# Gated unit of a two-layer encoder: seven products of quarters in place of eight

## The chip, the cores and the metric

The kernel runs on one core of a Trainium2 chip. The metric is the device time of one execution in microseconds. TensorE (PE) does the matmuls and reads its weights through a separate load (PEld). VectorE (DVE), ScalarE (ACT) and GpSimd (POOL) do the elementwise work, and SyncE (SP) issues every transfer, in order.

## The reference, cut to what matters

The input x has 1024 tokens of 1024 channels in float32. Layer 0 runs a state-space branch (S5) and a retention branch side by side; layer 1 is a convolution module. The changed part is the gated unit at the end of the S5 branch:

```python
y = jax.nn.gelu(y)
y = y * jax.nn.sigmoid(y @ glu_w + glu_b)      # 1024 x 1024 weights
...
y_s5 = y_s5 * jax.nn.silu(g_s5)
y_ret = retention(q, k, v) * jax.nn.silu(g_ret)
return jnp.concatenate([y_s5, y_ret], axis=-1) @ w_out
```

## The kernel before, in words

Channels lie on the 128 partitions and tokens along the free axis, in two halves of 512. A block is 128 channels, so 1024 channels are eight blocks. Each float32 product is made of three matmuls: every operand is split into a rounded high part and the rest as a low part, and `mm3` (L161) issues high x high, high x low and low x high into one PSUM bank. `gemm` (L171) does so for the eight k-blocks: 24 matmuls of 128x512 for an output block of one token half.

Weights come through `wnext`, `wload` and `wload_pieces` (L109 to L160): one block of 512 KB at a time, loaded into `wf`, rounded to `wh` by ACT (L158), and its low part `wl` made by GpSimd, or by DVE for some names (L159). Each of the three has three buffers, and `wnext` issues loads two blocks ahead along the list that `plan` writes out.

The retention (`retention`, L864) runs four pairs of heads. `ret_proj` projects k and q, multiplies them out of PSUM into `kraw` and `qraw` (DVE, L913), and `turn` rotates them: four swap transfers into `swp`, products on GpSimd (L926, L928), an addition on DVE (L929). `ret_heads` then transposes k, evicts it as `kt` (L998), forms the states (`kv`, L1015), the scores (`sp`), masks them (`sc`, L1038), and makes the outputs `ro`, normalises them and stores them to `yr_d`. `y_pass` (L855) rides along, two blocks a pair: it loads the S5 output from `y_d`, applies gelu on ACT (L861) and stores it to `yn_d`.

The gated unit (L1141 to L1155) follows. Its operands, the blocks of `yn_d`, are loaded through the weight staging buffers and split into 16 + 16 tiles of `opA` (tag `A0` for the first token half, `A1` for the second) as soon as the last value projection lets those tiles go; low parts of the second half stand behind the last pair's `kt` and first mask. For each of eight output blocks and two halves, `gemm` fills one of three `mm` banks. Beside it SP loads `yg` (the SiLU gate, two buffers) and `yn` (three buffers), and GpSimd multiplies them (L1146). Then ACT takes tanh of the bank (L1150) into `sg`, DVE multiplies (L1151), ACT rounds the half of it to the high part (L1153) and DVE makes the low part (L1154). At the end the retention output is loaded from `yr_d` and split into the same `opA` tiles, and `w_out` (L1163) multiplies both by their halves of the output projection, an output block at a time.

The order of instructions on each engine is set by a planner that simulates the program: it takes ready work by program order, and `issue_after(x)` keeps what it encloses behind x.

## Time and profile before

| | us |
|---|---|
| median of 3 runs | 1202.06 (1201.37 to 1202.63) |
| the profiled execution | 1200.1 |
| its span, first to last instruction | 1198.3 |
| PE, DVE, ACT, POOL busy | 1188.7, 802.9, 477.8, 638.0 |
| first and last matmul of the gated unit start | 547.0, 646.0 |

The granted TensorE clock was 0.999 of full speed. Matmul records overlap one another, so a busy PE is not a measure of its rate; the starts of following matmuls are. In windows and timelines times are counted from the start of the span.

### The profile page before, as it was taken

The numbers are of one execution on the slowest core, as the hardware profiler recorded it, in microseconds if no ns is written. First come the engines' busy times: TensorE is split into PE (matmuls) and PEld (weight loads), VectorE is DVE, ScalarE is ACT, GpSimd is POOL, SyncE is SP. The second block draws the span as 40 slices with busy tenths as digits, with TensorE's granted clock in tenths as the row PEclk, the third lists the DMA queues.
The fourth block names the chain that finished last, engine by engine and source line by source line (L and its number), as shares of the span: only waits on it lengthen the run. The fifth ranks groups of instructions, "written<-read, shape, count | busy, mean of one in ns | idle before, by whom it ended". The sixth has DMA issues, their size and how long they took to land.

```text
span 1198.3 us, 17247 instructions
## 1 busy us (share of the span) xinstructions
PE 1188.7 (99%) x6424; PEld 996.2 (83%) x6424; DVE 802.9 (67%) x1388; ACT 477.8 (40%) x700; POOL 638.0 (53%) x442
## 2 busy tenths in 40 slices
PE   9999999999999999999999999999999999999997
PEld 7788888888888889998888888888888888888877
DVE  7975798777421557447655332599999799999533
ACT  6322232223223223144335322545535575434563
POOL 2059999987146254242441110678453567757643
PEclk9999999999999999999999999999999999999999
DMA  9344355564395175477547885765678654356774
GB/s 349 99 137 135 123 165 179 175 180 160 108 290 176 53 220 156 152 215 255 163 148 260 307 270 195 247 210 207 210 251 277 206 185 157 117 178 230 239 278 154
DMA packets 105220, 234.19 MB, mean 195 GB/s; under 512 B 9520, under 2 KB 40112, under 8 KB 104496
## 3 DMA queue, kind: packets, MB, share of 16 engines
q1 hardware_dynamic: 105136, 233.09, 59.2%
q8 instruction: 50, 0.82, 0.3%
q14 instruction: 34, 0.28, 0.1%
HBM read 166.80 MB, written 62.06 MB: 191 GB/s over the span
## 4 chain that ended last, share of the span: by engine, by line
PE 95%; DVE 2%; ACT 1%; DMA 1%; issue 1%; POOL 0%; SPq 0%; DVEq 0%; POOLq 0%; ACTq 0%
PE mm_g L167 8%; PE mm_g L168 7%; PE mm_g L169 7%; PE mm_wo L169 5%; PE mm_wo L167 5%; PE mm_wo L168 5%; PE mm_glu L167 2%; PE mm_b L168 2%; PE mm_b L169 2%; PE mm_glu L169 2%; PE mm_a L168 2%; PE mm_a L169 2%; PE mm_glu L168 2%; PE mm_b L167 2%; PE mm_a L167 2%; PE mm_oc L168 2%
## 5 line engine op out<-in xcount | busy, mean ns | idle before, releaser
L1274 DVE SCALAR_TENSOR_TENSOR cv<-u,convw,cv 128x512 f32<-128x512 f32 x398 | 273.3, 749 | 11.9 <-ACT cv L1260 9.6
L1254 POOL TENSOR_TENSOR tp<-tp,tp 128x512 f32<-128x512 f32 x64 | 82.9, 1296 | 44.1 <-ACT tp L1253 43.1
L167 PE MATMUL mm_g<-xh,wh_g 128*128 128x512 f32 x256 | 101.8, 398 | 0.0
L169 PE MATMUL mm_g<-xh,wl_g 128*128 128x512 f32 x256 | 100.1, 391 | 0.0
L168 PE MATMUL mm_g<-xl,wh_g 128*128 128x512 f32 x256 | 100.0, 391 | 0.0
L1253 ACT ACTIVATE tp<-u,convw 128x512 f32<-128x512 f32 x64 | 45.7, 720 | 35.3 <-POOL tp L1254 33.6
L396 POOL TENSOR_TENSOR s1q<-s1q,s1q 128x512 f32<-128x512 f32 x12 | 17.3, 1438 | 78.6 <-ACT s1q L391 78.6
L167 PEld LDWEIGHTS mm_g<-xh,wh_g 128*128 128x128 f32 x256 | 48.0, 188 | 11.7 <-issue 1.2
L169 PEld LDWEIGHTS mm_g<-xh,wl_g 128*128 128x128 f32 x256 | 48.0, 188 | 10.4
L168 PEld LDWEIGHTS mm_g<-xl,wh_g 128*128 128x128 f32 x256 | 48.1, 188 | 9.9 <-issue 0.4
L168 PE MATMUL mm_oc<-zl,wh_woc 128*128 128x512 f32 (+1 forms) x152 | 54.4, 360 | 0.5 <-POOL zl L1099 0.5
L169 PE MATMUL mm_oc<-zh,wl_woc 128*128 128x512 f32 (+1 forms) x152 | 53.9, 358 | 0.2 <-DMA wl_woc<-lo_woc 0.2
L167 PE MATMUL mm_oc<-zh,wh_woc 128*128 128x512 f32 (+1 forms) x152 | 54.1, 361 | 0.0
L1146 POOL TENSOR_TENSOR yg<-yg,yn 128x512 f32<-128x512 f32 x16 | 22.0, 1379 | 57.9 <-DMA yg<-gs_d 21.1
L352 DVE TENSOR_TENSOR gt<-mm_g,R 128x512 f32<-128x512 f32 x32 | 21.8, 682 | 43.6 <-PE mm_g L169 43.6
L167 PE MATMUL mm_g<-h1h,wh_cg 128*128 128x512 f32 x128 | 50.4, 394 | 0.0
L167 PE MATMUL mm_glu<-yh,wh_glu 128*128 128x512 f32 x128 | 50.3, 393 | 0.0
L167 PE MATMUL mm_wo<-yrh,wh_wor 128*128 128x512 f32 x128 | 50.2, 392 | 0.0
L167 PE MATMUL mm_b<-h1h,wh_cb 128*128 128x512 f32 x128 | 50.2, 392 | 0.0
L169 PE MATMUL mm_a<-h1h,wl_ca 128*128 128x512 f32 x128 | 50.2, 392 | 0.0
L169 PE MATMUL mm_wo<-yrh,wl_wor 128*128 128x512 f32 x128 | 49.9, 390 | 0.0
L168 PE MATMUL mm_b<-h1l,wh_cb 128*128 128x512 f32 x128 | 49.9, 390 | 0.0
(415 smaller groups left out, 3610.9 us busy)
## 6 DMA issues: line engine op xcount, KB each, us to landing
wf_g<-w_ab SPq DMA_DIRECT2D x16, 512.0 KB
wf_wos<-w_out SPq DMA_DIRECT2D x16, 512.0 KB
wf_wor<-w_out SPq DMA_DIRECT2D x16, 512.0 KB
wf_cb<-w_c SPq DMA_DIRECT2D x16, 512.0 KB
wf_ca<-w_c SPq DMA_DIRECT2D x16, 512.0 KB
wf_woc<-w_out_c SPq DMA_DIRECT2D x16, 512.0 KB
wf_v<-w_v SPq DMA_DIRECT2D x12, 512.0 KB
wf_cg<-w_c SPq DMA_DIRECT2D x11, 512.0 KB
```

What stands on the lines that cost most here:

```text
L167: nc.tensor.matmul(ps, wh[:, kb, :], xh, start=start, stop=False)
L168: nc.tensor.matmul(ps, wh[:, kb, :], xl, start=False, stop=False)
L169: self.last_mm = nc.tensor.matmul(ps, wl[:, kb, :], xh, start=False, stop=stop)
L352: nc.vector.tensor_tensor(gt[:, c], ps[:], self.R[:, c], op=ALU.mult)
L396: nc.gpsimd.tensor_tensor(a, a, sq[:], op=ALU.add)
L1146: gp.tensor_tensor(yg[:], yg[:], yn[:], op=ALU.mult)
L1253: nc.scalar.mul(sk[:], u[:, k:k + HALF], cw[:, nb, k:k + 1])
L1254: gp.tensor_tensor(s0[:], s0[:], sk[:], op=ALU.add)
L1274: v.scalar_tensor_tensor(dst[:], *tap, accs_[i][:], op0=ALU.mult, op1=ALU.add)
```

## The change

The 1024 x 1024 weights are cut into four quarters of 512 x 512, and y into four quarters: two halves of channels (b1., b2.) by two halves of tokens (b.1, b.2). The product is then formed by Winograd's variant of Strassen's scheme: seven products of quarters, with sums of quarters as operands, instead of eight. One product of quarters is four output blocks by four k-blocks, 48 `mm3` matmuls, for one token half's worth of 512 columns.

What is moved, added and removed:

- The weight list holds 14 blocks in place of 8: two (`m`) for each of seven products. A block of 512 KB now holds two output blocks (`a`) by four k-blocks, so it serves 24 matmuls in place of 48. Eight of the 14 are sums, read from a DRAM buffer `ws_d`; six are quarters as given.
- `glu_sums` makes the sums of the weights: for each of four groups two loads of 512 KB, four DVE operations of 128x512, two stores of 512 KB. Two groups come in the first pair and two in the third. They use the `swp` and `raw` buffers between rotations, and their DVE work stands behind the last raw eviction.
- `y_pass` handles blocks k and k + 4 together: k = 0 and 1 in the first pair, 2 in the third, 3 in the fourth, none in the second. After the gelu, DVE forms four sums of 128x512 and splits two results of 128x1024 into high and low parts, which are stored in `t_d` (four stores of 512 KB). The split of k = 1 stands behind the first pair's second mask.
- The retention's mask and k decay are loaded per pair.
- The gated unit runs the products in the order 1, 2 (both halves m), 6, 7, 4, then 5 and 3. Products 1 and 2 share their banks, as do 5 and 3; product 1 is copied out by ACT (`u2`) before product 2 is added. Products 6 and 7 are added to `u2` and `u3` by DVE, product 4 is subtracted from `u3` in a spare bank. `gated` works in the bank: tanh, DVE product and half are all written to PSUM or read from it, but for two blocks.
- The operands t1 to t4 come ready split from `t_d` (eight loads of 256 KB each); y11, y21 and y22 are loaded from `yn_d` and split as before.
- `w_out`'s first block takes its k-blocks in plain order.

```diff
-        seq += [(A["w_glu"][nb], f"glu{nb}") for nb in range(8)]
+        self.ws_d = self.dram.tile([2, 2, P, 2, KB, P], F32, name="ws_d")
+        quad = lambda i, j, m: A["w_glu"][i, m, :, j]
+        sums = lambda n, m: self.ws_d[n // 2, m, :, n % 2]
+        glu = [q for m in range(2) for q in (quad(0, 0, m), quad(0, 1, m))]
+        glu += [q(m) for q in (lambda m: sums(0, m), lambda m: sums(2, m), lambda m: quad(1, 1, m)) for m in range(2)]
+        glu += [sums(n, m) for m in range(2) for n in (3, 1)]
+        seq += [(q, f"glu{i}") for i, q in enumerate(glu)]
...
+    def mm3(self, ps, w, kb, x, start, stop, more=False):
...
-    def y_pass(self, rp, cb):
+    def y_pass(self, rp, k):
         nc = self.nc
-        yt = rp.tile([P, 8, P], F32, name=f"yp_{cb}", tag="yp", bufs=1)
-        nc.sync.dma_start(yt[:], self.y_d[cb].rearrange("i h g m -> (h g) i m"))
-        yn = rp.tile([P, P, 8], F32, name=f"yn_{cb}", tag="ynt", bufs=1)
-        nc.scalar.activation(yn[:], yt[:].rearrange("p i m -> p m i"), AF.Gelu_apprx_tanh)
-        nc.sync.dma_start(self.yn_d[cb * P:(cb + 1) * P], yn[:].rearrange("p m i -> p (m i)"))
+        yns = []
+        for i, cb in enumerate((k, k + 4)):
+            yt = rp.tile([P, 8, P], F32, name=f"yp_{cb}", tag="yp", bufs=1)
+            nc.sync.dma_start(yt[:], self.y_d[cb].rearrange("i h g m -> (h g) i m"))
+            yn = rp.tile([P, P, 8], F32, name=f"yn_{cb}", tag="ynt", bufs=2)
+            nc.scalar.activation(yn[:], yt[:].rearrange("p i m -> p m i"), AF.Gelu_apprx_tanh)
+            yn = yn[:].rearrange("p m i -> p (m i)")
+            nc.sync.dma_start(self.yn_d[cb * P:(cb + 1) * P], yn)
+            yns.append(yn)
+        (b11, b12), (b21, b22) = ((y[:, :HALF], y[:, HALF:]) for y in yns)
+        v = nc.vector
+        with self.tc.issue_after(self.last_raw.ins):
+            v.tensor_tensor(b22, b22, b12, op=ALU.subtract)
+            v.tensor_tensor(b12, b12, b11, op=ALU.subtract)
+            v.tensor_tensor(b11, b22, b11, op=ALU.add)
+            v.tensor_tensor(b21, b11, b21, op=ALU.subtract)
+        yield
+        for i in range(2):
+            hi = rp.tile([P, T], F32R, name=f"th{i}_{k}", tag="yp", bufs=1)
+            v.tensor_copy(hi[:], yns[i])
+            v.tensor_tensor(yns[i].bitcast(F32R), yns[i], hi[:].bitcast(F32), op=ALU.subtract)
+            nc.sync.dma_start(self.t_d[i, 0, k * P:(k + 1) * P], hi[:].bitcast(F32))
+            nc.sync.dma_start(self.t_d[i, 1, k * P:(k + 1) * P], yns[i])
+    def glu_sums(self, g, tag):
+        nc, v = self.nc, self.nc.vector
+        m, c = g // 2, slice(g % 2 * 4, g % 2 * 4 + 4)
+        q = [self.rq.tile([P, T], F32, name=f"gs{i}_{g}", tag=tag, bufs=2)[:].rearrange("p (j n) -> p j n", j=2)
+             for i in range(2)]
+        for i in range(2):
+            nc.sync.dma_start(q[i], self.A["w_glu"][i, m, :, :, c].rearrange("p j k n -> p j (k n)"))
+        (a11, a12), (a21, a22) = ((t[:, 0, :], t[:, 1, :]) for t in q)
+        with self.tc.issue_after(self.last_raw.ins):
+            v.tensor_tensor(a22, a21, a22, op=ALU.add)
+            v.tensor_tensor(a21, a11, a21, op=ALU.subtract)
+            v.tensor_tensor(a11, a22, a11, op=ALU.subtract)
+            v.tensor_tensor(a12, a12, a11, op=ALU.subtract)
+        with self.tc.issue_after(self.last_swap.ins):
+            for i in range(2):
+                nc.sync.dma_start(self.ws_d[i, m, :, :, c].rearrange("p j k n -> p j (k n)"), q[i])
     def retention(self, st):
         nc, A = self.nc, self.A
...
+            for g, tag in (((0, "swp"), (1, "raw")), (), ((2, "swp"), (3, "raw")), ())[pair]:
+                self.glu_sums(g, tag)
...
-                for cb in (2 * pair, 2 * pair + 1):
-                    self.y_pass(rq, cb)
+                parts = [self.y_pass(rq, k) for k in ((0, 1), (), (2,), (3,))[pair]]
+                for i, p in enumerate(parts):
+                    next(p)
+                    if i == 0:
+                        next(p, None)
+            if pair == 0:
+                with self.tc.issue_after(self.masked[1].ins):
+                    next(parts[1], None)
+        mask = rp.tile([P, 2, P], F32, name=f"retmask_{pair}", tag="retmask", bufs=2)
+        nc.sync.dma_start(mask[:], A["ret_mask"][:, 2 * pair:2 * pair + 2])
+        kdec = rp.tile([P, 2, 64], F32, name=f"kdec_{pair}", tag="kdec", bufs=2)
+        nc.sync.dma_start(kdec[:], A["ret_kdec"][:, 2 * pair:2 * pair + 2])
...
-        ys_in = load_split(self.yn_d, "y", False)
-        for nb, h in [(nb, h) for nb in range(6) for h in range(2)] + [(6, 0), (7, 0), (6, 1), (7, 1)]:
-            ps = self.bank(f"mm_glu{nb}_{h}", aux=False)
-            self.gemm(ps[:], ws[nb], ys_in[h])
-            sg = lp.tile([P, HALF], F32, name=f"sg{nb}_{h}", tag="u", bufs=5)
-            v.scalar_tensor_tensor(sg[:], sg[:], 1.0, yg[:], op0=ALU.add, op1=ALU.mult)
-            glu_end = v.scalar_tensor_tensor(b[:], sg[:], 0.5, a[:].bitcast(F32), op0=ALU.mult, op1=ALU.subtract)
-        yr = load_split(self.yr_d, "yr", True)
+        def load_split(parts, name, h, wide, behind=None):
+            res = []
+            for i, part in enumerate(parts):
+                if wide:
+                    if i % 2 == 0:
+                        f2 = self.wp.tile([P, 2, HALF], F32, name=f"{name}f{i}", tag="wf", bufs=3)
+                    f = f2[:, i % 2, :]
+                else:
+                    f = lp.tile([P, HALF], F32, name=f"{name}f{i}", tag="tp", bufs=3)[:]
+                nc.sync.dma_start(f, part)
+                a, b = (self.op_tile(self.opA, f"A{h}", f"{name}{q}{i}") for q in "hl")
+                self.split(f, a, b, v, behind)
+                res.append((a, b))
+        B = lambda j, h: [self.yn_d[rows(4 * j + k), hs(h)] for k in range(4)]
+        def load_sum(name, i, c, h):
+            res = []
+            for k in range(4):
+                ops = [self.op_tile(self.opA, f"A{h}", f"{name}{q}{k}") for q in "hl"]
+                for j, o in enumerate(ops):
+                    nc.sync.dma_start(o[:].bitcast(F32), self.t_d[i, j, rows(k), hs(c)])
+                res.append(ops)
+            return res
+        b11, b21 = load_split(B(0, 0), "y11", 0, True), load_split(B(1, 0), "y21", 0, True, self.masked[0])
+        u2 = [lp.tile([P, HALF], F32, name=f"gu2_{n}", tag=tag, bufs=1) for n, tag in enumerate(("cq", "cs", "pilot", "sq"))]
+        u3 = [opB.tile([P, HALF], F32, name=f"gu3_{n}", tag="B1") for n in range(4)]
+        nw = iter(range(14))
+        wn = lambda: self.wnext(f"glu{next(nw)}")
+        def product(ps, w, a, x, more=False):
+            for k in range(4):
+                self.mm3(ps[:], w, 4 * a + k, (x[k][0][:], x[k][1][:]), k == 0 and not more, k == 3, more)
+        def gated(nb, h, z):
+            src = z
+            if h == 0 and nb < 2:
+                z = lp.tile([P, HALF], F32, name=f"sg{nb}_{h}", tag="u", bufs=5)
+            nc.scalar.activation(z[:], src[:], AF.Tanh, scale=0.5, bias=hgb[:, nb:nb + 1])
+            v.scalar_tensor_tensor(z[:], z[:], 1.0, yg[:], op0=ALU.add, op1=ALU.mult)
+            nc.scalar.mul(a[:], z[:], 0.5)
+            return v.scalar_tensor_tensor(b[:], z[:], 0.5, a[:].bitcast(F32), op0=ALU.mult, op1=ALU.subtract)
+        def spare(name, n):
+            return ps_cv.tile([P, HALF], F32, name=name, tag=("cv", "cn")[n % 2])
+        for m in range(2):
+            pss = [self.bank(f"mm_glu1{2 * m + a}", aux=False) for a in range(2)]
+            for i, x in ((1, b11), (2, b21)):
+                w = wn()
+                if i == 1:
+                    t2, t3 = (load_sum("yt2", 0, 0, 1), None) if m == 0 else (t2, load_sum("yt3", 1, 1, 1))
+                for a in range(2):
+                    product(pss[a], w, a, x, i == 2)
+                    if i == 1:
+                        nc.scalar.copy(u2[2 * m + a][:], pss[a][:])
+                    else:
+                        gated(2 * m + a, 0, pss[a])
+        t4 = load_sum("yt4", 1, 0, 0)
+        for i, x in ((6, t2), (7, t3), (4, t4)):
+            for m in range(2):
+                w = wn()
+                for a in range(2):
+                    n = 2 * m + a
+                    ps = spare(f"mm_glu{i}{n}", n) if i == 4 else self.bank(f"mm_glu{i}{n}", aux=False)
+                    product(ps, w, a, x)
+                    if i == 4:
+                        v.tensor_tensor(ps[:], u3[n][:], ps[:], op=ALU.subtract)
+                        gated(4 + n, 0, ps)
+                    else:
+                        v.tensor_tensor((u2 if i == 6 else u3)[n][:], u2[n][:], ps[:], op=ALU.add)
+            if i == 6:
+                t1, b22 = load_sum("yt1", 0, 1, 0), load_split(B(1, 1), "y22", 1, False)
+        for m in range(2):
+            pss = [self.bank(f"mm_glu5{2 * m + a}", aux=False) for a in range(2)]
+            for i, x in ((5, t1), (3, b22)):
+                w = wn()
+                for a in range(2):
+                    n = 2 * m + a
+                    product(pss[a], w, a, x, i == 3)
+                    if i == 5:
+                        z = spare(f"mm_gluz{n}", n)
+                        v.tensor_tensor(z[:], u3[n][:], pss[a][:], op=ALU.add)
+                        gated(4 + n, 1, z)
+                    else:
+                        v.tensor_tensor(pss[a][:], u2[n][:], pss[a][:], op=ALU.add)
+                        glu_end = gated(n, 1, pss[a])
+        yr = [load_split([self.yr_d[rows(k), hs(h)] for k in range(KB)], f"yr{h}", h, False) for h in range(2)]
...
-                if nb == 0:
-                    seq.append(seq.pop(KB - 1))
```

54 lines of the change are left out of this document (15 added, 39 removed).

## The prediction

> **What bounds the kernel now.** I read the page first: its busy shares, then its chain of work that ended last.
>
> ```profile
> span 1198.3 us, 17247 instructions
> ...
> PE 1188.7 (99%) x6424; PEld 996.2 (83%) x6424; DVE 802.9 (67%) x1388; ACT 477.8 (40%) x700; POOL 638.0 (53%) x442
> ...
> PE 95%; DVE 2%; ACT 1%; DMA 1%; issue 1%; POOL 0%; SPq 0%; DVEq 0%; POOLq 0%; ACTq 0%
> ```
>
> TensorE is busy 99% of the span and carries 95% of the chain. A busy PE alone proves little, since matmul records overlap; the timeline gives the pace, and the rows of the gated unit's tile the count (min/median/max ns, first and last start).
>
> ```profile
> 598.66 0.39 PE L167 MATMUL mm_glu<-yh,wh_glu 128*128 128x512 f32 x1
> ...
> 604.10 0.39 PE L167 MATMUL mm_glu<-yh,wh_glu 128*128 128x512 f32 x1
> L167 PE MATMUL mm_glu<-yh,wh_glu x128: 389/389/504, 547.0 to 645.6; 128*128 128x512 f32 x128
> ```
>
> The two timeline rows stand 24 matmuls apart: 5.44 us, so one starts every 0.2267 us although each record is 0.39 us long. With the two other products of the three-term form, as many each, the gated unit has 3 x 128 = 384 matmuls, 87.0 us of TensorE. The windows show what else runs in that stretch and in the retention pairs before it; the columns are busy us of PE, PEld, DVE, ACT and POOL, the granted clock, the share of the DMA engines and GB/s.
>
> ```profile
> 470.00:490.00 20.00, 20.00 (x169) 19.91 (x168) 4.41 (x6) 6.91 (x10) 5.68 (x5) 1.00 0.88 286
> 490.00:510.00 20.00, 20.00 (x165) 17.00 (x164) 13.19 (x57) 2.66 (x6) 4.57 (x3) 1.00 0.18 54
> 530.00:550.00 20.00, 20.00 (x158) 19.47 (x157) 9.97 (x13) 10.40 (x19) 5.39 (x3) 1.00 0.55 170
> 547.00:581.00 34.00, 34.00 (x236) 28.73 (x235) 26.93 (x82) 11.61 (x19) 11.96 (x7) 1.00 0.67 234
> 603.00:636.00 33.00, 33.00 (x147) 27.35 (x146) 17.36 (x16) 12.05 (x19) 13.85 (x9) 1.00 0.53 170
> 670.00:690.00 20.00, 20.00 (x89) 16.54 (x89) 5.45 (x5) 4.26 (x6) 3.24 (x2) 1.00 0.95 347
> ```
>
> Before, every engine but PE has room while the gated unit runs, and the transfers are about half busy. That room is what the change spends.
>
> **Fewer matmuls.** Seven products of four row blocks by four k-blocks by three are 7 x 4 x 12 = 336 matmuls instead of 384. 48 x 0.2267 us = 10.9 us leave TensorE. No matmul is added: all sums are on VectorE. The later stages take what the gated unit delivers, the convolution's DVE chain among them, so a gain here moves everything behind it as a whole. So -10.9 us is the most that can come, and all else is what is given back.
>
> **Sums in the retention pairs.** Per pair of y blocks (four in all): four subtractions or additions of 128x512, then two copies and two subtractions of 128x1024. Per quarter of the weights (four): four of 128x512. That is 32 operations of 512 and 16 of 1024. Rows for the nearest operations:
>
> ```profile
> L929 DVE TENSOR_TENSOR krot<-krot,kswp x8: 681/1763/1778, 354.5 to 524.6; 128x512 f32<-128x512 f32 x8
> L159 DVE TENSOR_TENSOR wl_wor<-wf_wor,wh_wor x8: 1216/1224/1970, 644.2 to 718.0; 128x1024 fp32r<-128x1024 f32 x8
> 489.25 1.29 DVE L998 TENSOR_TENSOR kt<-ktp,kdec 128x512 f32<-128x512 f32 x2 [9.50 <-PE ktp L996]
> 494.35 1.75 PE L1015 MATMUL kv<-v,kt 128*64 128x128 f32 x28
> ```
>
> At the low ends 32 x 0.68 + 16 x 1.22 = 41 us, at the high ends 32 x 1.78 + 16 x 1.97 = 88 us, spread over three pairs. The tightest is the third: eight weight sums and one y pair, 12 x 0.68 + 4 x 1.22 = 13.0 us, or 12 x 1.76 + 4 x 1.97 = 29 us if every one collides with GpSimd. DVE has 20 - 4.4 = 15.6 us free in 470-490. GpSimd is busy 5.7 of those 20 us, so about 28% of the sums collide: 13.0 + 0.28 x 16 = 17.5 us, 1.9 us over. Queued behind them on DVE is the kt eviction at 489.25; PE wants kt for kv at 494.35, and kt's two operations take 1.29 us, so 3.8 us of delay are covered by the k projection that PE runs meanwhile. Above that PE loses it. Bounds: 0 (later operands can't make PE earlier) and 29 - 15.6 - 3.8 = 9.6 us; I take 0.5, since the 1.9 us are inside the cover. The transfers of that pair (2 MiB weights in, 2 MiB out, 2 MiB of y sums out, 6.3 MB) meet a DMA share of 0.88 in 470-490 but 0.18 in 490-510, so they end by 510 at the latest. The SP queue gains them too, and a store there holds back the loads behind it until DVE is done; weights are kept two blocks ahead, 2 x 5.44 us where a block has 24 matmuls, so I price that at 0 to 2 us and take 0.5.
>
> The same row of the rotation's addition shows what lies between the ends: 0.68 us alone, 1.76 us when GpSimd multiplies rotations beside it, both inputs in SBUF. The Trainium skill ("SBUF — State Buffer", Who interferes with whom) has the rule for it: a VectorE operation with two SBUF inputs and a GpSimd operation that reads SBUF exclude each other, and the second waits for the whole of the first. It speaks against sums of SBUF operands beside GpSimd work; by it the third pair goes towards the rival of colliding sums below. The trace agrees on the mechanism (0.68 against 1.76 us).
>
> **Start of the gated unit.** The first product (y11, 12 matmuls for each of two blocks) needs only operands that came early before. The second needs y21, whose low parts stand behind the last pair's first mask.
>
> ```profile
> 556.85 0.68 DVE L1038 TENSOR_TENSOR sc<-sp,retmask 128x512 f32<-128x512 f32 x1
> 557.45 1.28 DVE L1099 TENSOR_TENSOR yl<-yf,yh 128x512 fp32r<-128x512 f32 x2
> 564.07 0.48 PE L167 MATMUL mm_glu<-yh,wh_glu 128*128 128x512 f32 x1
> ```
>
> Two low parts took 1.28 us there, four take 2.6, done by 560.1, and PE comes back from the heads at 564.07. Cost 0; at worst, with nothing but kv (1.75 us) between the first product, begun at 547.0, and the second, PE loses 560.1 - 547.0 - 5.4 - 1.8 = 5.9 us. The ACT copy of the first product out of its bank hides under the other block's 12 matmuls, 2.72 us. The last pair's y sums are 4 x 0.68 + 4 x 1.22 = 7.6 us, and DVE has 10 of 20 us free in 530-550; also 0.
>
> **The gates.** These rows give the pieces of a gate and of the weights beside it (count, then busy us and mean ns).
>
> ```profile
> L1150 ACT ACTIVATE sg<-mm_glu,hgb 128x512 f32<-128x512 f32 x15 | 10.3, 683 | 10.1 <-PE mm_glu L169 10.1
> L1151 DVE SCALAR_TENSOR_TENSOR sg<-sg,yg 128x512 f32<-128x512 f32 x14 | 14.5, 1032 | 18.8 <-ACT sg L1150 15.5 <-POOL yg L1146 3.2
> L1153 ACT ACTIVATE ysh<-sg 128x512 fp32r<-128x512 f32 x14 | 8.5, 629 | 14.6 <-DVE sg L1151 14.6
> L1154 DVE SCALAR_TENSOR_TENSOR ysl<-sg,ysh 128x512 fp32r<-128x512 f32 x14 | 16.5, 1191 | 5.7 <-ACT ysh L1153 5.6
> L1146 POOL TENSOR_TENSOR yg<-yg,yn 128x512 f32<-128x512 f32 x16 | 22.0, 1379 | 57.9 <-DMA yg<-gs_d 21.1 <-DMA yn<-yn_d 8.9 <-issue 7.0
> L159 POOL TENSOR_TENSOR wl_glu<-wf_glu,wh_glu 128x1024 fp32r<-128x1024 f32 x7 | 18.5, 2644 | 11.5 <-ACT wh_glu L158 11.5
> L1174 DVE TENSOR_TENSOR x<-mm_wo,xr x16: 684/691/692, 660.3 to 910.0; 128x512 f32<-128x512 f32 x16
> ```
>
> DVE: two operations a gate, 16 x (1.03 + 1.19) = 35.5 us before. Gated in the bank, one input is in PSUM; the nearest row for that is L1174, 0.69 us and steady, so 16 x 1.38 + 20 new additions x 0.69 = 35.9 us: no more than before. POOL: six more weight blocks, 6 x 2.64 = 15.9 us, beside 57.9 us of idle: no bound over the stage.
>
> The pace is the question. A gate came every 24 matmuls, 5.44 us; from the fourth product's two weight blocks on, twelve come every 12 matmuls, 2.72 us. Each gate turns over one of two yg buffers: free, load, GpSimd product, DVE product.
>
> ```profile
> 577.86 0.38 SPq L1143 DMA_DIRECT2D yg<-gs_d  x1
> ...
> 581.65 1.29 POOL L1146 TENSOR_TENSOR yg<-yg,yn 128x512 f32<-128x512 f32 x1 [4.24 <-DMA yg<-gs_d]
> 589.84 0.32 SPq L1143 DMA_DIRECT2D yg<-gs_d  x1
> ...
> 593.05 1.29 POOL L1146 TENSOR_TENSOR yg<-yg,yn 128x512 f32<-128x512 f32 x1 [4.38 <-DMA yg<-gs_d]
> ```
>
> The load takes 3.2 to 3.8 us; with 1.29 and 0.69 and 0.5 for the hand-overs (an estimate: ysl has 5.6 us of idle behind ACT over 14 operations, 0.4 each) a turn is 5.7 to 6.3 us against the 5.44 us in which PE wants it. PE feels it first at the second bank of the last pair of blocks, which waits for the seventh of the twelve gates: three turns late, 3 x 0.3 to 3 x 0.9 = 0.8 to 2.6 us. That gate's chain is an addition, tanh, product, half, low part: 0.69 + 0.68 + 0.69 + 0.63 + 0.69 + 0.6 = 4.0 us, of the 5.44 us until its bank is wanted, so 1.4 us are covered. PE waits 0 to 1.2 us; with the load at 5 us, as more traffic would make it, a turn is 7.5 us and PE waits 3 x 2.06 - 1.4 = 4.8 us. I take 3 us, between the two, because the traffic does rise:
>
> ```profile
> DMA packets 7821, 17.58 MB, mean 198 GB/s; under 512 B 863, under 2 KB 991, under 8 KB 7816
> ...
> yg<-gs_d SPq DMA_DIRECT2D x15, 256.0 KB
> wf_glu<-w_glu SPq DMA_DIRECT2D x6, 512.0 KB
> ```
>
> That is 547-636 us before. The change adds 32 loads of 256 KB (the sums of y) and six weight blocks of 512 KB, 11.5 MB: 29.1 MB in the 89 us that are left, 327 GB/s. The fullest row of the trace, 670-690, is 347 GB/s at a share of 0.95, that is 365 at a full one: it fits, at nine tenths.
>
> The Trainium skill ("DMA: Bandwidth & Descriptors", Specifications) states about 358 GB/s of HBM for a core. By it the sum stays under the limit too; the row of 347 is near it, but no run here shows the limit itself.
>
> **The sum.** -10.9 + 0.5 (kt) + 0.5 (SP) + 3 (gates) = -6.9 us. The profiled execution took 1200.1 us, 1.8 us around its span; the median of the runs is 1202.06, 1.96 above it. So 1193.2 profiled, 1195.2 as a median. About 0.2%, 2.4 us, is what a measurement of this kernel can tell from no change.
>
> **Rivals.** *Transfers become the bound (slower).* In the last 32.6 us of the gated unit's matmuls fall twelve gates' loads (6 MiB), six weight blocks (3 MiB, two of them of the next stage) and half of the retention operands (2 MiB): 11.5 MB, 354 GB/s of 365. If the sums for the fourth and fifth products and the last quarter of y (5 MiB, 5.2 MB) have not landed by then, because SP issues in order and stood behind a buffer, 16.8 MB need 45.9 us: 13.3 us of waiting, which alone eats the gain. With 1 MiB more of retention operands (2.9 us) and the 1 us of kt and SP it is 1200.1 - 10.9 + 13.3 + 2.9 + 1 = 1206.4 profiled, 1208.4 as a median. It turns the sign from 4.9 MB carried over on. For it: SP does wait in order for such buffers.
>
> ```profile
> SPq L1145 <- POOL yg L1146: 40.5, 13, 6.2
> ```
>
> 40.5 us in 13 waits, up to 6.2 us. Against: the operand buffers of the first two products are free four weight blocks, 21.8 us, before that stretch begins. Chance 0.25.
>
> *The gain is given back.* Turns of the yg buffers of 9 us, each behind half a burst of eight loads (2.1 MB, 5.7 us at 365 GB/s): 3 x 3.56 - 1.4 = 9.3 us, with 1 us of the rest -0.6 us, 1201.5. Chance 0.12.
>
> *The sums collide.* Each meets GpSimd: 9.6 us at kt in the third pair, with 3.5 us of the rest 1202.06 - 10.9 + 13.1 = 1204.3. Against it stand POOL's 5.7 busy us of 20. Chance 0.05.
>
> *The arithmetic doesn't shrink.* If the 48 matmuls were made up elsewhere, time would stay at 1202 or above. The code adds none; 0.01, counted as no change.
>
> **The numbers.** Forecast 1195.2, its own range 1190.5 (all kept, less the 0.7 us by which runs differ) to 1199.5, chance 0.57. No change 0.13, slower 0.30. For 8 in 10 the range goes up into the slower case, to 1209; above lie more bursts that collide, about 0.13, and below 1190.5 about 0.04. Runs of before lie between 1201.37 and 1202.63.
>
> **What would show it.** Right: 336 mm_glu matmuls at 0.2267 us; PE idle inside the gated unit under 6 us, put down to a bank, a gate or yg, in its last third; the retention pairs without PE idle over 2 us; DVE gate products at 0.69 us; a DMA rate above 300 GB/s from the second product to the first output block. Wrong: PE idle of over 9 us ahead of the fifth or third product put down to a load of sums or of weights; kv or a raw eviction late in the third pair; or new idle behind the gated unit, where I see none.

## The result, and the profile after

The changed kernel takes 1212.34 us (median of 4 runs, 1210.8 to 1213.59) against 1202.35 for the kernel before: a ratio of 1.0084, 95% interval 1.0066 to 1.0101. It is slower by 10 us; the forecast was 1195.2, in a range up to 1209.0. The profiled execution took 1212.6 us.

The page of the changed kernel, its span, the busy shares and the chain:

```profile
span 1210.8 us, 17395 instructions
...
PE 1184.4 (98%) x6376; PEld 990.9 (82%) x6376; DVE 850.9 (70%) x1452; ACT 482.5 (40%) x706; POOL 654.1 (54%) x448
...
PE 79%; DMA 8%; DVE 6%; ACT 2%; issue 2%; SPq 1%; POOL 0%; DVEq 0%; POOLq 0%; ACTq 0%
```

PE's share of the chain fell from 95 to 79%, and the shares of DMA and DVE rose from 1 and 2 to 8 and 6%. 48 matmuls are gone and the rest keep their pace: the timeline rows of two matmuls of product 4 that stand 24 apart give 5.43 us, 0.226 each.

```profile
619.10 0.39 PE L174 MATMUL mm_glu<-yt4h,wh_glu 128*128 128x512 f32 x1
...
624.53 0.39 PE L174 MATMUL mm_glu<-yt4h,wh_glu 128*128 128x512 f32 x1
```

So the 10.9 us did leave TensorE, and 12.5 + 10.9 = 23.4 us of the span came back in other ways. Where they came back is read from first starts: of the output projection before (the gated unit's first is 547.0), then of the gated unit and the output projection in the changed kernel.

```profile
L167 PE MATMUL mm_wo<-ysh,wh_wos x128: 389/389/478, 646.3 to 903.7; 128*128 128x512 f32 x128
...
L174 PE MATMUL mm_glu<-y11h,wh_glu x16: 389/389/504, 558.0 to 587.0; 128*128 128x512 f32 x16
L174 PE MATMUL mm_wo<-ysh,wh_wos x128: 389/389/792, 652.6 to 915.1; 128*128 128x512 f32 x128
```

The gated unit starts 11.0 us later. It then takes 97.3 us in place of 99.3 (94.6, and 2.7 for twelve of its matmuls that come after the first of the output projection), so 8.9 of its 10.9 us are lost inside it. What stands behind it takes 3.5 us longer. Most of this stands in the waits of PE (us in total, times, longest); the first line is the longest wait of the kernel before, the others are of the changed kernel.

```profile
PE idle L258 <- DVE mhalf L204: 1.1, 1, 1.1
...
PE ktp L1051 <- ACT v L1038: 6.5, 1, 6.5
PE mm_wo L174 <- DVE ysl L1226: 2.7, 1, 2.7
PE mm_glu L174 <- DVE ysl L1226: 2.3, 2, 1.2
PE kv L1070 <- DVE kt L1053: 2.0, 1, 2.0
PE ro L1114 <- DVE sc L1093: 1.4, 1, 1.4
...
PE mm_oc L176 <- DMA wl_woc<-lo_woc: 0.9, 2, 0.6
PE mm_b L174 <- DVE x L1288: 0.9, 1, 0.9
PE mm_glu L174 <- DVE gu L1255: 0.8, 1, 0.8
```

But for 0.9 us at mm_oc, the releasers in these lines are ScalarE and VectorE, not the DMA queue. Why ScalarE was late at ktp is read from its timeline in the first pair (in brackets the idle time before, and what ended it):

```profile
394.15 2.05 ACT L872 ACTIVATE yn<-yp 128x1024 f32<-128x1024 f32 x1 [1.94 <-DMA yp<-y_d]
396.11 1.03 ACT L164 CAST wh_q<-wf_q 128x1024 fp32r<-128x1024 f32 x1
401.69 1.94 ACT L872 ACTIVATE yn<-yp 128x1024 f32<-128x1024 f32 x1 [4.55 <-issue]
403.52 2.42 ACT L1038 ACTIVATE v<-mm_v,Rtok 128x512 f32<-128x512 f32 x4
```

SP issued that last load of y into `yp` at 396.64; there is one `yp` buffer, and the gelu before it ended at 396.2. ScalarE takes its work in a fixed order, so the four value evictions, whose matmuls had ended at about 396, stood behind a gelu that waited for its load (the profile names no releaser for it; 5.05 us lie between the issue of that load and the gelu). They held their banks, and the transposes into ktp had none. The windows show a second cost (columns as in the prediction: the granted clock is the third number from the end).

```profile
400.00:405.00 5.00, 0.74 (x4) 0.74 (x5) 0.00 (x0) 3.31 (x4) 0.00 (x0) 0.79 0.54 193
405.00:410.00 5.00, 5.00 (x14) 3.98 (x13) 3.35 (x2) 3.16 (x4) 2.58 (x1) 0.53 0.49 165
410.00:415.00 5.00, 5.00 (x55) 4.11 (x54) 4.36 (x11) 0.00 (x0) 0.00 (x0) 1.00 0.35 103
```

After the idle time TensorE runs at a granted clock of 0.79 and 0.53 for ten us. From the second half of ktp (404.26) to kv (411.73) it took 7.5 us. It took 5.1 us before, so that is 2.4 us more:

```profile
397.13 0.60 PE L996 MATMUL ktp<-ident,krot 128*128 128x128 f32 x4
...
402.23 1.75 PE L1015 MATMUL kv<-v,kt 128*64 128x128 f32 x28
```

The Trainium skill ("TensorE: Matmul & The Clock Gate", Part 1: The HAM clock gate) says that the clock halves after an idle window of about 3.4 us and comes back after a busy one. The 0.53 agrees with it.

In the gated unit, the groups of VectorE by line cost what was forecast (0.69 us an operation in PSUM), and the transfers fill the DMA engines (share 1.04 in the window below):

```profile
L1222 DVE SCALAR_TENSOR_TENSOR mm_glu<-mm_glu,yg 128x512 f32<-128x512 f32 x10 | 6.9, 695 | 6.8 <-ACT mm_glu L1221 4.3 <-POOL yg L1216 2.4
L1226 DVE SCALAR_TENSOR_TENSOR ysl<-mm_glu,ysh 128x512 fp32r<-128x512 f32 x10 | 6.8, 685 | 0.2 <-DMA yr_d<-grl 0.2
```

```profile
595.00:605.00 10.00, 8.02 (x34) 5.99 (x33) 5.56 (x7) 4.70 (x7) 4.63 (x2) 1.00 1.04 393
```

### The profile page after: what moved, and what is told of

Its sections match the earlier page's. It is cut to its first block, busy times and chain, and to the rows that moved or that the text cites. A ratio compares the mean times of both kernels' runs of the same rounds, so it can differ in the third digit from the quotient of the medians.

```text
span 1210.8 us, 17395 instructions
## 1 busy us (share of the span) xinstructions
PE 1184.4 (98%) x6376; PEld 990.9 (82%) x6376; DVE 850.9 (70%) x1452; ACT 482.5 (40%) x706; POOL 654.1 (54%) x448
## 4 chain that ended last, share of the span: by engine, by line
PE 79%; DMA 8%; DVE 6%; ACT 2%; issue 2%; SPq 1%; POOL 0%; DVEq 0%; POOLq 0%; ACTq 0%
PE mm_g L174 7%; PE mm_g L175 7%; PE mm_g L176 7%; PE mm_wo L174 5%; PE mm_wo L175 5%; PE mm_wo L176 5%; PE mm_b L174 2%; PE mm_b L175 2%; PE mm_b L176 2%; PE mm_a L176 2%; PE mm_a L175 2%; PE mm_a L174 2%; PE mm_oc L175 2%; PE mm_oc L176 2%; PE mm_oc L174 2%
## 5 line engine op out<-in xcount | busy, mean ns | idle before, releaser
L165 POOL TENSOR_TENSOR wl_glu<-wf_glu,wh_glu 128x1024 fp32r<-128x1024 f32 x14 | 34.9, 2494 | 41.7 <-ACT wh_glu L164 37.6
L174 PE MATMUL mm_wo<-ysh,wh_wos 128*128 128x512 f32 x128 | 50.6, 396 | 2.7 <-DVE ysl L1226 2.7
L165 POOL TENSOR_TENSOR wl_v<-wf_v,wh_v 128x1024 fp32r<-128x1024 f32 x12 | 30.8, 2567 | 39.7 <-ACT wh_v L164 39.7
L175 PE MATMUL mm_wo<-ysl,wh_wos 128*128 128x512 f32 x128 | 50.3, 393 | 0.0
L174 PE MATMUL mm_a<-h1h,wh_ca 128*128 128x512 f32 x128 | 50.2, 392 | 0.0
```

The costliest lines, as they stand in the source:

```text
L165: lo[i].tensor_tensor(wl[:].rearrange(fl)[:, c], wf[:, c], h.bitcast(F32), op=ALU.subtract)
L174: nc.tensor.matmul(ps, wh[:, kb, :], xh, start=start, stop=False, **more)
L175: nc.tensor.matmul(ps, wh[:, kb, :], xl, start=False, stop=False, **more)
```

## The experiments

Each was timed in 5 rounds beside the kernel before. In the table, us is (ratio - 1) x 1202, the distance from the kernel before. The profiled execution is one of the runs; waits on transfers vary between runs (the wait ahead of ktp, with the same code there, was 6.7, 6.5, 4.6, 4.6 and 4.4 us in five profiles), so verdicts go by the ratios and only the places by the profiles.

| run | ratio, 95% interval | us |
|---|---|---|
| the changed kernel | 1.0084 [1.0066, 1.0101] | +10.1 |
| products without sums | 1.0012 [1.0004, 1.0021] | +1.4 |
| sums without products | 1.0114 [1.0097, 1.0131] | +13.7 |
| second y pair later (e1) | 1.0045 [1.0033, 1.0058] | +5.4 |
| gelu behind values (e2) | 1.0089 [1.0073, 1.0104] | +10.7 |
| five yg buffers (e3) | 1.0079 [1.0065, 1.0093] | +9.5 |
| weight sums behind kt (e4) | 1.0107 [1.0092, 1.0123] | +12.9 |
| e1 and three more (g3) | 1.0054 [1.0040, 1.0069] | +6.5 |
| e1, half the sum loads (g4) | 1.0130 [1.0115, 1.0145] | +15.6 |
| changed kernel, banks free (i3) | 1.0033 [1.0019, 1.0046] | +4.0 |
| e1, banks free (h1) | 0.9989 [0.9980, 0.9998] | -1.3 |
| h1, sums behind masks (h2) | 1.0037 [1.0025, 1.0049] | +4.4 |
| products alone, banks free (h3) | 0.9956 [0.9944, 0.9968] | -5.3 |
| h1, masks ahead of splits (i1) | 0.9979 [0.9969, 0.9989] | -2.5 |
| i1, gelu in two (i2) | 0.9993 [0.9982, 1.0003] | -0.8 |
| i1, low parts behind sums (j1) | 0.9982 [0.9972, 0.9993] | -2.2 |

**The two halves of the change.** Products without sums (it leaves them out, and plain quarters stand in their place):

```diff
-            for g, tag in (((0, "swp"), (1, "raw")), (), ((2, "swp"), (3, "raw")), ())[pair]:
-                self.glu_sums(g, tag)
-                parts = [self.y_pass(rq, k) for k in ((0, 1), (), (2,), (3,))[pair]]
+                for cb in (2 * pair, 2 * pair + 1):
+                    self.y_pass(rq, cb)          # as in the kernel before
```

> The changed kernel without any sums: no sums of weights, no sums of y, no splits or stores of them; y goes two blocks a pair as in the kernel before. The gated unit is as in the changed kernel, 336 matmuls in the same order with as many loads of the same size, but its operands are plain quarters of y and of the weights in place of the sums. Theory A (the retention pairs lose 11 to 12 us to the sums, the gated unit 9 to its own waits): 1212.3 - 11.5 = 1200 to 1202, with the gated unit's waits (1.4, 0.9, 1.3, 1.2, 2.9) still there. Rival B (the gated unit loses most of it): 1207 or more. Rival C (without the sums the gated unit's waits go too, since they come from its late start): 1192 to 1195.

Sums without products:

```diff
+        ys_in = load_split(self.yn_d, "y", False)   # the gated unit of before, behind all the sums
```

> The kernel before with all the sums added and unused: the same loads, VectorE sums, splits and stores in the same retention pairs as in the changed kernel (its retention is that of the changed kernel), and the gated unit of before, 384 matmuls on plain y and plain weights. Theory A: 1202 + 11.5 = 1213 to 1214.5, with the idle ahead of ktp in the first pair (4.6 to 6.6 us) and ahead of kv in the third (2 us). Rival B (the gated unit loses most): 1205 or less. In rival C it is again 1213 or more, so C is told from A by the run without sums alone.

The products alone come out at +1.4, the sums alone at +13.7. Both lie a little above theory A and far from rival B, and the first is far from C too. Seven products gain 10.9 us of matmuls and lose 12.3 again, most of it inside the gated unit (in that profile 96.2 us to the first matmul of the output projection and 2.7 for twelve matmuls that come after it, 98.9; in the kernel before 99.3), with nothing of the sums there. That profile is of the slowest of its runs. The difference to the changed kernel, 8.7 us, is what the sums cost on top. The two do not add up to the changed kernel (15.1 against 10.1). A part of this shows in the profile of the second, which has a wait that the changed kernel has not, 2.9 us at the scores of the last pair, beside the two known ones; the rest stays open.

```profile
PE ktp L1046 <- ACT v L1033: 6.7, 1, 6.7
PE sp L1082 <- DVE S L1075: 2.9, 1, 2.9
PE kv L1065 <- DVE kt L1048: 2.0, 1, 2.0
```

**The first pair.** The second y pair moved to the second retention pair (e1), or left there with its loads and gelus behind the value evictions (e2):

```diff
-                parts = [self.y_pass(rq, k) for k in ((0, 1), (), (2,), (3,))[pair]]
+                parts = [self.y_pass(rq, k) for k in ((0,), (1,), (2,), (3,))[pair]]      # e1
+                    with self.tc.issue_after(self.last_v.ins) if i else nullcontext():    # e2
                         next(p)
```

> The changed kernel with its second pair of y blocks (k = 1: two loads, two gelus, sums, splits, stores) moved from the first retention pair to the second. Theory A (in the first pair one yp buffer and ScalarE's fixed order make the four value evictions stand behind the gelu of the eighth load; PE idles 6.5 us ahead of ktp and then runs at a granted clock of 0.79 and 0.53, 2.7 us more): the idle and the low clock go, ktp starts at 396.7 in place of 404.3, the whole falls by about 9, to 1203. Rival B (it is the amount of transfers and of VectorE work in the retention that costs, wherever it stands): the second pair gets an idle of several us ahead of kv or kt, and the time stays at 1209 to 1214.

> The changed kernel with the second y pair still in the first retention pair, but its loads and gelus standing in the order behind the last value eviction on ScalarE. It moves no byte to another pair. Theory A (ScalarE's order does it): the 6.5 us idle ahead of ktp and the low clock behind it go, 1203 to 1205; what the late pair's sums cost after that, at most 2. Rival B (amount of transfers and VectorE work in that pair): the wait moves to ktp or kv a few us later, 1209 or more.

e1 gains 4.7 us, half of what was expected, and lies between the two theories. In its profile ktp starts at 396.4 and the clock stays at 1.00; of the rest, 2 us were lost again by the time the gated unit began. e2 gains nothing, and its profile says why: ktp's wait falls to 0.7 us, and in its place PE waits for a mask, which on VectorE stands behind the sums that the late gelu feeds.

```profile
PE ro L1115 <- DVE sc L1094: 5.0, 2, 3.7
```

```profile
413.61 0.69 DVE L879 TENSOR_TENSOR yn<-yn,yn 128x512 f32<-128x512 f32 x1 [4.13 <-issue]
...
417.09 1.28 DVE L1094 TENSOR_TENSOR sc<-sp,retmask 128x512 f32<-128x512 f32 x2
```

The time is the one that rival B gave, but the wait went from ScalarE's queue to VectorE's, so neither theory holds as I had put it. An operation that waits for a transfer was put ahead of work that was ready, and a change of one queue's order left it ahead of work on the next.

There is a second transfer in this chain. The sums overwrite the gelu's tile, so they wait until its store to `yn_d` has landed. The changed kernel's row for that sum names it:

```profile
406.62 0.69 DVE L879 TENSOR_TENSOR yn<-yn,yn 128x512 f32<-128x512 f32 x1 [24.53 <-DMA yn_d<-yn]
```

Its gelu had ended at 403.6, 3.0 us earlier; in e2 the gelu ended at 410.9 and the sum came 2.7 us later. No run gave the sums a tile of their own, or the load of y a second `yp` buffer, so how the loss divides into order and late transfers is not shown.

**The third pair.** e4 puts the sums of weights behind kt:

```diff
-        with self.tc.issue_after(self.last_raw.ins):
+        with self.tc.issue_after(raw.ins if g < 2 else self.last_kt.ins):
```

> The changed kernel with the third pair's VectorE sums of weights and their stores behind that pair's kt eviction in place of ahead of it; loads as before. Theory A (kt stands behind a sum whose load takes 9.5 us): kv of the third pair comes 2.0 us earlier and the whole is 1210.3. Rival B (what is moved only collides with the mask and the next pair's raw eviction): an idle of 2 us or more turns up between kv and the fourth pair, 1212 or more. The first pair's 6.5 us and the gated unit's waits stay in both.

Rival B: 2.8 us above the changed kernel, with intervals that overlap. kv is nearly on time, and the state S stands behind the sums instead. PE also waits 2.0 us for a block of weights at the start of the gated unit, which the changed kernel does not.

```profile
PE sp L1094 <- DVE S L1087: 1.5, 1, 1.5
...
PE kv L1077 <- DVE kt L1060: 0.4, 1, 0.4
```

Order was not all that made kt late. In the changed kernel four sums stand right ahead of it. The first two took 1.70 and 2.77 us, with GpSimd at work on weights beside them, and the other two 0.69 each:

```profile
498.83 1.70 DVE L902 TENSOR_TENSOR gs<-gs 128x512 f32<-128x512 f32 x1 [1.58 <-DMA gs<-w_glu]
500.56 2.77 DVE L903 TENSOR_TENSOR gs<-gs,gs 128x512 f32<-128x512 f32 x1
...
499.94 2.84 POOL L165 TENSOR_TENSOR wl_v<-wf_v,wh_v 128x1024 fp32r<-128x1024 f32 x1
```

That is 3.1 us more than two sums of 0.69, against the 2.0 us that kv waited. No run takes GpSimd's work away from there, so the share of the collision is not shown.

**The gated unit.** The prediction had priced the turn of the yg buffers. e3 gives it five:

```diff
-            yg = lp.tile([P, HALF], F32, name=f"yg{nb}_{h}", tag="ld", bufs=2)
+            yg = lp.tile([P, HALF], F32, name=f"yg{nb}_{h}", tag="u", bufs=5)
```

> The changed kernel with the gate operand yg in five buffers (those of u, nearly idle in the gated unit) in place of two. Theory A (the turn of a yg buffer, load to GpSimd product to VectorE product, sets the pace of the last twelve gates): the waits of 1.2 us at 646.9 and 2.9 us at 652.6 and the clock of 0.71 behind them go, 1207 (by 5.5). Rival B (the transfers are full there and yg comes late in any buffer): the waits stay above 3 us, 1211 to 1213. In both the waits at 574.7, 597.7 and 601.9 stay.

No difference can be measured (1.0079 against 1.0084). In the profile the wait ahead of the output projection fell from 2.7 to 1.1 us, but that at product 6 grew to 2.1. g4 leaves out half the loads of the sums, and uses the high part as low part:

```diff
-                ops = [self.op_tile(self.opA, f"A{h}", f"{name}{q}{k}") for q in "hl"]
+                o = self.op_tile(self.opA, f"A{h}", f"{name}h{k}")
```

> The changed kernel with the second y pair in the second retention pair, and with the low parts of the sums of y not loaded in the gated unit: sixteen loads of 256 KB, 4.2 MB, are left out, and the high part is used in place of the low one. Matmuls, gates and their order stay. Theory A (the waits at products 6 and 3 and ahead of the output projection come from the order of work on VectorE and from yg): below 1.5 us gained, 1205 to 1206.5, the 3.2 us ahead of the output projection stay. Rival B (transfers are the bound in the gated unit): the waits at yt2 (0.9, 1.1) go and that ahead of the output projection falls below 1 us, 1200 to 1203.

It is 10 us slower than e1, which nobody expected. The planner wrote another order for it, so that it says nothing of the price of the transfers. But with 4.2 MB less to load, PE waited 4.0 and 3.4 us at two banks of mm_glu for VectorE. What holds those banks led to the next run. `gated` works in the bank, so that a bank is free only when the low part is made. The changed kernel's VectorE at product 6:

```profile
592.75 0.70 DVE L1222 SCALAR_TENSOR_TENSOR mm_glu<-mm_glu,yg 128x512 f32<-128x512 f32 x1 [2.70 <-ACT mm_glu L1221]
596.97 0.69 DVE L1255 TENSOR_TENSOR gu<-gu,mm_glu 128x512 f32<-128x512 f32 x1 [3.52 <-PE mm_glu L176]
598.04 0.70 DVE L1222 SCALAR_TENSOR_TENSOR mm_glu<-mm_glu,yg 128x512 f32<-128x512 f32 x1 [0.39 <-ACT mm_glu L1221]
598.65 2.36 DVE L1226 SCALAR_TENSOR_TENSOR ysl<-sg,ysh 128x512 fp32r<-128x512 f32 x2
601.18 1.31 DVE L1226 SCALAR_TENSOR_TENSOR ysl<-mm_glu,ysh 128x512 fp32r<-128x512 f32 x2 [0.17 <-DMA yr_d<-grl]
```

Two of the three mm banks are taken until the low parts `ysl<-mm_glu` from 601.18 on: one holds a gate from 592, the other product 2 until 596.5 and then its gate. Product 6 has one bank: it waits for gu to empty it (gu ends at 597.66, PE starts again at 597.71), and at 601.92 for the first low part. h1 takes the gates of blocks 0 to 3 out of their banks on top of e1, i3 does it in the changed kernel alone. Two of those eight gates were out already, so six move:

```diff
-            if h == 0 and nb < 2:
+            if h == 0 and nb < 4:
                 z = lp.tile([P, HALF], F32, name=f"sg{nb}_{h}", tag="u", bufs=5)
...
-                        v.tensor_tensor(pss[a][:], u2[n][:], pss[a][:], op=ALU.add)
-                        glu_end = gated(n, 1, pss[a])
+                        z = lp.tile([P, HALF], F32, name=f"sg{n}_1", tag="u", bufs=5)
+                        v.tensor_tensor(z[:], u2[n][:], pss[a][:], op=ALU.add)
+                        glu_end = gated(n, 1, z)
```

> The changed kernel with the second y pair in the second retention pair, and with the eight gates of output blocks 0 to 3 worked in SBUF tiles instead of in their mm banks: tanh (first token half) or the addition (second half) writes the tile, and the bank is free after that one operation. The gates in spare banks stay. Theory A (a gate held in its bank keeps it for about 4 us longer, so that product 6 and the last blocks run on one free bank of three): the waits for gu at yt2 (0.9) and for ysl at yt2, yt1 and ahead of the output projection (1.1, 0.8, 3.2) and the low clock behind the last go, 5 to 7 us, 1200 to 1201.5 against 1206.5. Rival B (the yg turn sets the pace, or VectorE's load, which grows by about 0.4 us an operation with two SBUF inputs): the waits stay over 4 us in sum, 1205 or more.

> The changed kernel with nothing else but the eight gates of blocks 0 to 3 out of their banks; both first y pairs stay in the first retention pair. Theory A (the retention's loss and the gated unit's add up): 1212.3 - 5.4 = 1206 to 1208, the 4.6 to 6.6 us ahead of ktp stay, the waits of 0.9, 1.3, 1.2 and 2.9 in the gated unit go. Rival B (the bank gain was that of a schedule shifted by the second y pair's move): 1210 or more.

Theory A in both: 6.7 us from e1 to h1, 6.1 from the changed kernel to i3. The waits for ysl are gone from both lists; of those for a bank this is left in h1:

```profile
PE sp L1083 <- DVE S L1076: 1.8, 1, 1.8
PE ro L1110 <- DVE sc L1089: 1.5, 2, 1.3
...
PE mm_glu L174 <- DVE gu L1251: 0.6, 1, 0.6
```

All transfers are still there, yg still has two buffers, and gates in SBUF cost VectorE more (1.06 us a product in place of 0.70), which the profile of h1 shows in its groups. From e1 to h1 and from the changed kernel to i3 it is nearly the same gain, so the bank and the first pair add up: 4.7 + 6.1 = 10.8, against 11.4 from the changed kernel to h1. The products alone gain as much (h3, with y21's low parts behind the mask too):

> The run without any sums (plain quarters as operands, 1202.5), with the gates of blocks 0 to 3 out of their banks and y21's low parts behind the second mask. It has nothing of the sums in the retention. Theory A (the gated unit gives its 10.9 us back to gates in banks, 5 to 7, and to y21 and the clock, 3): 1193 to 1195. Rival B (the yg turn or the transfers): 1199 or more.

It comes out at -5.3 us against the kernel before, between the two theories, and its profile still has 1.8 us of wait for gu. Half of the 10.9 us is the most that seven products brought in any run here.

**What stands ahead of a mask.** g3 (with five yg buffers, the yr low parts behind the last gate, y21's behind the second mask), h2 and i1 move operations of VectorE behind masks:

```diff
-        b11, b21 = load_split(B(0, 0), "y11", 0, True), load_split(B(1, 0), "y21", 0, True, self.masked[0])
+        b11, b21 = load_split(B(0, 0), "y11", 0, True), load_split(B(1, 0), "y21", 0, True, self.masked[1])   # g3, h2, h3, i1
...
-        with self.tc.issue_after(self.last_raw.ins):
+        with self.tc.issue_after(self.masked[1].ins if k in (1, 2) else self.last_raw.ins):   # h2: the sums
...
+            if pair == 1:                            # i1: one split
+                with self.tc.issue_after(self.masked[1].ins):
+                    next(parts[0], None)
```

> The changed kernel with four changes of order and buffers: the second y pair in the second retention pair (as in the run that moved it), yg in five buffers, the low parts of the retention operands yr of the first token half behind the last gate on VectorE, and the low parts of y21 behind the second of the last pair's masks. Against 1206.5 with the first of them alone. Theory A (late in the gated unit VectorE is in series: 6.4 us of yr low parts and the yg turns stand between the gates; early in it y21's low parts stand ahead of a mask): the waits of 3.2, 0.8 and 1.3 us and the clock of 0.66 and 0.83 behind them go, 6 to 8 us, 1199 to 1201. Rival B (the transfers set those waits): the waits come back at other gates, less than 2 us gained, 1205 or more.

> As the run with the gates out of their banks, and besides y21's low parts behind the second of the last pair's masks, and the y sums of the second and third retention pairs behind those pairs' second masks, so that no sum stands ahead of kt, S or a mask there. Theory A (VectorE's order, where sums that wait for a late load stand ahead of the heads' operations, costs 2 us in the second pair, and y21 1.3 us and a clock of 0.83 behind it, 1.7): 3 to 5 us less than the run it builds on, 1195 to 1198, faster than the kernel before. Rival B (transfers late by 5 to 9 us only shift the wait): a raw eviction or an output of the heads waits instead, less than 1 us gained.

> The run with the gates out of their banks (1201.1), with two steps of VectorE put behind masks: y21's low parts behind the last pair's second mask, and in the second pair the second split of y (it waits for a store to free its one buffer) behind that pair's second mask. Nothing else is deferred, so that the gelus keep their times. Theory A (an operation that waits for a transfer and stands ahead of S or a mask on VectorE costs what it waits): the 1.8 us at sp in the second pair and the 1.5 us at ro in the last go, 1197 to 1199. Rival B (any such move costs as much elsewhere, as where all sums were deferred, 1206): 1200 or more.

g3 and h2 fall to their rivals. In h2 the deferred sums keep their buffers, so the fourth pair's loads of y come later (the last is issued at 531.9, in h1 at 521.5), and in that pair the value evictions stand behind a gelu once more:

```profile
PE mm_v L1016 <- ACT v L1019: 6.1, 1, 6.1
```

i1 moves only what stood ahead, and no gelu. The waits at sp and ro are gone from its list (in this profile kv of the third pair waits 1.9 us); by the ratios it gains 1.2 us over h1, with intervals that just overlap. It has the lowest ratio of the versions that compute the whole: 1199.26 us, 0.9979 [0.9969, 0.9989], faster than both kernels. Two steps beyond it, the gelu in halves (i2) and the low parts of y22 and of the first gates behind gu (j1), bring nothing that can be measured:

```diff
+            for m in (slice(0, 64), slice(64, P)):       # i2
...
+            b22 = load_split(B(1, 1), "y22", 1, False, last_gu)   # j1, and ysh, ysl of blocks 0 to 3 behind gu
```

> The run before this in the list, with each gelu of 128x1024 in two of half the width on ScalarE, so that value evictions of the third and fourth pairs can go between. Theory A (value evictions stand behind a gelu of 2.1 us): of the 1.4 us in which the value products wait about 1 goes, 0.5 to 1 us less than the run before. Rival B (they stand behind its wait for the load): no difference, within 0.5 us.

> The run with the masks ahead of the splits (1199.3), with the low parts that stand ahead of the additions of products 6 and 7 (gu) on VectorE put behind them: those of the first four gates behind the last gu of product 7, those of y22 behind the last gu of product 6. Theory A (VectorE's fixed order: in that run a low part waits 3.4 us for a store of the retention output, and gu, and with it the bank for product 7, stands behind it): the 2.2 us wait for gu and the clock of 0.66 behind it go, 1196 to 1197.5. Rival B (the transfers of that stretch, share 1.05, hold the operands too): PE waits for operands of product 7 or 4 instead, 1198.5 or more.

In i1's profile a low part that waits for a store stands ahead of gu, and PE waits 2.2 us for it:

```profile
600.21 2.24 DVE L1228 SCALAR_TENSOR_TENSOR ysl<-sg,ysh 128x512 fp32r<-128x512 f32 x1 [3.44 <-DMA yr_d<-grl]
602.38 2.87 DVE L1156 TENSOR_TENSOR y22l<-y22f,y22h 128x512 fp32r<-128x512 f32 x1
605.18 0.67 DVE L1257 TENSOR_TENSOR gu<-gu,mm_glu 128x512 f32<-128x512 f32 x1
```

In that of j1 the wait is down to 0.4 us, but the medians are 1199.26 and 1198.89. Whether i1's other runs have that wait at all, one profile can't say. So its theory is shown for the place and not for the time, which is the one its rival gave.

## Why the prediction was wrong

**The arithmetic** (-10.9) was right: 336 matmuls at 0.226 us.

**The sums in the retention** (0.5, bounds 0 to 9.6) were the first step that failed. They cost 8.7 us (the changed kernel against the products alone). I had priced one place, kt in the third pair: it cost 2.0 us of wait, inside the bounds, though I had taken it as covered. My share of 28% that collides was a mean over 20 us; of the four sums right ahead of kt two ran long. The first pair, with two y pairs and two groups of weights, got no price at all, and it lost most, 6.5 us of wait and 2.4 of clock in the profiled run; e1, which moves a y pair away, gains 4.7 by the ratios. I had counted busy time on VectorE and room on its windows; what decided in the first pair was the place of operations that wait for a load in the fixed order of ScalarE and VectorE. The prediction asked who stands behind kt; it did not ask who stands behind a gelu. e2, e4 and h2 show that the question has to be asked again for every engine after each move.

**SP's stores** (0.5): no wait in PE's list is put down to a load of weights in the retention.

**The start of the gated unit** (0, at worst 5.9): 1.4 us at ro, since y21's low parts stood ahead of a mask. The y21 group took 6.1 us for four, 1.54 each, where I had used 0.64; GpSimd worked from 568.25 to 574.04.

```profile
568.68 4.24 DVE L1154 TENSOR_TENSOR y21l<-y21f,y21h 128x512 fp32r<-128x512 f32 x2 [0.21 <-ACT y21h L1152]
572.84 0.68 DVE L1093 TENSOR_TENSOR sc<-sp,retmask 128x512 f32<-128x512 f32 x1
```

**The gates** (3, bounds 0 to 4.8) were the second step that failed, in its size and in its mechanism. I had priced the turn of the yg buffers; e3 shows that it is worth nothing measurable. The price of a gate in its bank I had taken from VectorE's durations alone, which were right (0.69), and I had tested the banks only at the last pair of blocks. The bank is held through tanh, product, half and low part, and through every operation that stands between them. That costs 6 us (i3: 6.1; e1 to h1: 6.7), part of it at product 6, in the middle.

**The sum** gave back 4.0 us (0.5 + 0.5 + 3). By the ratios 21.0 us came back: 8.7 by the sums and 12.3 without them. Of the 12.3, the banks and y21's place are worth 6.7 (products alone to h3).

**The rivals.** "Transfers become the bound" gave a time close to the measured one, 1208.4, but that is chance, for it is not what happened: h1 keeps every transfer and is faster than the kernel before (by 1.3 us, just clear of noise). That transfers land late has its part in several waits, though: the last load of y in the first pair took 5 us. My ceiling of 365 GB/s was too low, as the row of 393 shows; the kernel before already moved 418 GB/s for 2.2 us of the gated unit. The traffic itself came out below my sum, 26.7 MB at 300 GB/s from 558 to 647, where I had 29.1 and 327. "The sums collide" named GpSimd, and long operations beside it are there, at y21 and ahead of kt; they don't reach the first pair's loss, where PE waited for ScalarE. Of the signs named for being wrong, kv late in the third pair came, and also small waits behind the gated unit: 0.9 us at mm_b and 0.9 at mm_oc.

**Still open:** about 2 us behind the gated unit (1.7 to 2.4 in the profiles with the banks free), the waits just named among them; how the retention's loss divides into order, late transfers and collisions; and the rest of the 5.6 us of the 10.9 that h3 does not bring.

## What to carry to other kernels

When work is added to an engine with room, list what stands behind each added operation that waits for a transfer, and on every engine that the operation feeds; the room in a window says nothing of that. When an operation is to be done in PSUM to save time on VectorE, count for how long the bank is held and by how much the matmuls' rotation shrinks: two longer operations in SBUF were worth 6 us here. And take a headline change apart first: the products alone were at +1.4 us and so had their own trouble, whatever the sums did.

## What the hardware showed

The granted clock also fell after a shorter wait. In e1 PE waited 1.3 us up to 565.4 and was busy for 8.3 of the 10 us before; the window 565 to 570 has a clock of 0.67.

```profile
555.00:560.00 5.00, 4.30 (x51) 3.35 (x46) 4.08 (x10) 0.99 (x2) 0.00 (x0) 1.00 1.04 386
560.00:565.00 5.00, 4.00 (x32) 3.20 (x32) 4.39 (x3) 3.38 (x6) 4.82 (x3) 1.00 1.06 399
565.00:570.00 5.00, 4.57 (x31) 4.45 (x32) 5.00 (x23) 0.60 (x2) 0.90 (x1) 0.67 1.03 372
```

The changed kernel waited as long at the same place (1.4 us up to 573.6), but had been busy for all of 560 to 570, and its clock stayed at 1.00 in the window behind. The Trainium skill (the same page and section as above) asks for an idle window of about 3.4 us; here shorter idle time was enough in one run and not in another. The 4.57 busy us at 0.67 are 1.5 us more than at full clock, so a wait of over a microsecond may cost as much again.
